# Output projection of the last chunk with the mixes as the stationary side

## The chip, the core and the metric

The kernel runs on one core of a Trainium2 chip. A core has a matrix engine (TensorE, PE in the profile; its loads of the stationary operand are shown as PEld), a vector engine (VectorE, DVE), a scalar engine (ScalarE, ACT), GpSimd (POOL) and SyncE (SP), which here only issues DMAs. Each of them works through its own queue in order; semaphores tie them together. The metric is the device time of one execution in microseconds (us); the profile comes from one execution of its own.

## The reference

One layer of a decoder with two groups of heads. For 1024 prompt tokens and 8 decode tokens (1032 rows in all, model width 2048) it computes an RMS norm, one wide input projection, sparse attention (1024 wide) and an mLSTM (1024 wide), gates both and sends them through one output projection:

```
mix = concatenate([attention * silu(z_att), mlstm_normed * sigmoid(o) * silu(z_ml)])   # (1032, 2048)
x   = x + mix @ w_out                                                                  # w_out (2048, 2048)
y   = x * rsqrt(mean(x * x, axis=-1) + 1e-6) * final_norm_w                            # final RMS norm
```

All of it is in float32. The caches, the attention and the mLSTM are not touched by the change and stay out here.

## The kernel before

Everything is kept transposed: features on the 128 partitions, tokens along the free dimension. `proj` (L1336) runs the input projection over 61 column tiles; lanes of jobs (L283 to L289) slip the attention and the mLSTM in between by weights and due times of their own. Both write to DRAM: the gates to `gateS`, attention to `attS`, the mLSTM to `hS`. After column tile 58 twelve of the sixteen mix row tiles (`PRE`) of the first token chunk are already made.

**float32 by halves.** A product of float32 operands is made from three matmuls: each operand is split into a high part H in the matrix format (a cast on ACT, L210) and a low part L (what the cast lost, a subtraction on DVE, L211); the products H·H, H·L and L·H are added in PSUM. `wload` and `wsplit` (L201, L215) load a weight tile of 128 x 512 numbers (256 KB) by one DMA on SP into a raw tile and make H and L of it. How far this runs ahead is set by the number of raw tiles and of pairs H, L in a pool: 2 and 3 in `wst`, 4 and 4 in `pb`.

**The output projection** (L1451 to L1483) walks through three token chunks `CB` = columns 0 to 387, 388 to 775, 776 to 1031. For each chunk `mixprep` makes the sixteen mix tiles (gate times branch output, split into mH and mL); those of `PRE` lie in pool `pb0`, used by chunks 0 and 2, the others in `pb`. Then for each of 16 tiles t of 128 output features, and four weight tiles of four row tiles each, 48 matmuls run with the **weights as the stationary side** (128 x 128) and the **mix as the moving side** (388 or 256 columns), L1470. The sum in one PSUM bank gets the residual added on DVE (L1475), is squared on ACT (L1478), and the squares are added up on GpSimd (L1480).

`finish` (L1430) ends a chunk. Because features lie on partitions, the sum of squares needs matmuls with a column of ones (`row_rstd`, L235), a power on GpSimd (L244), and transposes that spread the result over the partitions (L251, copied by L253). Then all 16 tiles y are scaled by norm weight and root (L1442; in the last chunk partly by ACT and GpSimd, L1444 and L1445) and stored to `yT` (L1446). `finish` is a generator: for chunks 0 and 1 it is advanced between the tiles t of the next chunk; for the last chunk it runs after everything else.

**What sets the order.** The code gives a program order; the framework then schedules each engine's queue against a simulated timeline, with everything under `tc.high_priority()` (weights) first. An instruction that is ready in that simulation may stand far ahead of its place in the code; the finished queues are then fixed and in order. Pools that are closed give their memory to later ones, and a tile on reused memory waits for the last reader of the old one.

Of the kernel before, what the change touches and what calls it, by code (L numbers as in the profile page):

```python
# [8 lines left out]
F32 = mybir.dt.float32  # L9
# [15 lines left out]
CB = ((0, 388), (388, 388), (776, 256))  # L25
CBN = 388
PRE = (8, 9, 10, 11, 12, 13, 14, 15, 0, 1, 2, 3)
# [110 lines left out]
def body(tc, A, stop=None):  # L138
# [62 lines left out]
    def wload(src, cols, pool, raws, bufs):  # L201
        raw = pool.tile([128, 4, 128], F32, name="wraw", bufs=raws)
        H = pool.tile([128, 4, 128], F32R, name="wH", bufs=bufs)
        L = pool.tile([128, 4, 128], F32R, name="wL", bufs=bufs)
# [10 lines left out]
    def wsplit(src, cols, pool, raws, bufs, tie=False):  # L215
        H, L, load, cast = wload(src, cols, pool, raws, bufs)
        dma = load(slice(0, 4))
        if tie:
            pin(dma)
        cast(slice(0, 4))  # L220
        return H, L

    evp = ctx.enter_context(tc.tile_pool(name="evp", bufs=6))
# [1072 lines left out]
    def mixload(ci, k, pool, tie=False):  # L1296
        c0, cn = CB[ci]
        nb = 2 if pool is not pb0 and k not in PRE else 1
# [124 lines left out]
    with tc.tile_pool(name="pb", bufs=2) as pb:  # L1423
        pre = PRE
        korder = pre + tuple(k for k in range(KT) if k not in pre)

        def ytile(ci, t):
            return pb.tile([128, CBN], F32, name=f"y{t}", bufs=2 if t < 3 else 1)[:, :CB[ci][1]]

        def finish(ci, ys, accs):  # L1430
            c0, cn = CB[ci]
            last = ci == len(CB) - 1
            rs = pb.tile([128, CBN], F32, name="rs", bufs=1)[:, :cn]
            rr = row_rstd(accs, rs, cn, pb)
            next(rr)
            yield
            for _ in rr:
                pass
            for t in range(KT):
                eng = G if last and t % 3 == 2 else V  # L1440
                if eng is V:
                    V.scalar_tensor_tensor(ys[t], ys[t], fnw[:, t:t + 1], rs, OP.mult, OP.mult)  # L1442
                else:
                    SC.activation(ys[t], ys[t], AF.Copy, scale=fnw[:, t:t + 1])  # L1444
                    G.tensor_tensor(ys[t], ys[t], rs, OP.mult)  # L1445
                (SC if last and t % 2 else SY).dma_start(A["yT"][t, :, c0:c0 + cn], ys[t])  # L1446
                if t % 4 == 3:
                    yield

        todo = None  # L1450
        for ci, (c0, cn) in enumerate(CB):  # L1451
            for k in korder:
                if mixb[ci][k] is None:
                    use0 = k in pre and ci % 2 == 0
                    mixprep(ci, k, pb0 if use0 else pb)
            ys = []
            acc = pb.tile([128, CBN], F32, name="acc", bufs=2)[:, :cn]
            for t in range(KT):
                p = bank()[:, :cn]
                n = 0  # L1460
                for q in range(4):
                    with tc.high_priority():
                        i = t * 4 + q
                        old = (ci == 0 and t == 0) or (i % 7) % 2 == 1
                        H, L = wsplit(A["wo"][t, q], 128, *((wst, 2, 3) if old else (pb, 4, 4)))
                    for k in range(4):
                        kk = korder[q * 4 + k]
                        mH, mL = mixb[ci][kk]
                        for w_, x_ in ((H, mH), (H, mL), (L, mH)):
                            PE.matmul(p, w_[:, k, :], x_, start=(n == 0), stop=(n == 47))  # L1470
                            n += 1
# [12 lines left out]
        for _ in todo:  # L1484
            pass
# [70 lines left out]
```

## Time and profile before

| What | Time |
|---|---|
| median of three runs | 2077.87 us (2075.32 to 2081.95) |
| the profiled execution | 2064.6 us |
| its span, first to last instruction | 2062.8 us |
| mean granted TensorE clock | 0.996 |
| TensorE matmuls busy | 2034.1 us (99%) |
| VectorE busy | 1215.2 us (59%) |
| ScalarE busy | 836.4 us (41%) |
| GpSimd busy | 331.5 us (16%) |
| DMA, mean over the span | 132 GB/s, 272.85 MB |

A row of a timeline gives start, duration, engine, line of the code, operation, output and inputs, shape, and in brackets the idle time before it and what ended it. Rows marked SPq are DMA issues, with the time the queue was occupied, not the time of the transfer. A matmul's duration includes its way through the array; consecutive ones overlap. A row of the groups gives count, busy time in us, mean of one in ns and, behind the second bar, the engine's idle time before them with its releasers.

### The profile page before, as it was taken

The numbers are of one execution on the slowest core, as the hardware profiler recorded it, in microseconds if no ns is written. First come the engines' busy times: TensorE is split into PE (matmuls) and PEld (weight loads), VectorE is DVE, ScalarE is ACT, GpSimd is POOL, SyncE is SP. The second block draws the span as 40 slices with busy tenths as digits, with TensorE's granted clock in tenths as the row PEclk, the third lists the DMA queues.
The fourth block names the chain that finished last, engine by engine and source line by source line (L and its number), as shares of the span: only waits on it lengthen the run. The fifth ranks groups of instructions, "written<-read, shape, count | busy, mean of one in ns | idle before, by whom it ended". The sixth has DMA issues, their size and how long they took to land.

```text
span 2062.8 us, 36440 instructions
## 1 busy us (share of the span) xinstructions
PE 2034.1 (99%) x13284; PEld 1999.7 (97%) x13284; DVE 1215.2 (59%) x3060; ACT 836.4 (41%) x1667; POOL 331.5 (16%) x405
## 2 busy tenths in 40 slices
PE   8999999999999999999999999989999999999997
PEld 8999999999999999999999999989999999999997
DVE  8332457556695876886455455356676467374464
ACT  8122244233531455312365555434454235343343
POOL 0002556600000000024011001012222111101011
PEclk9999999999999999999999999999999999999998
DMA  7444533322222212254322332256665758586584
GB/s 244 106 110 116 157 108 113 107 75 72 78 68 74 72 59 71 63 168 136 107 75 86 107 98 70 72 158 190 189 198 161 190 194 273 150 249 182 148 256 138
DMA packets 229777, 272.85 MB, mean 132 GB/s; under 512 B 36661, under 2 KB 162741, under 8 KB 229597
## 3 DMA queue, kind: packets, MB, share of 16 engines
q1 hardware_dynamic: 222381, 256.70, 42.0%
q0 software_dynamic: 5632, 12.59, 2.2%
q8 instruction: 104, 1.70, 0.4%
q10 hardware_dynamic: 1584, 1.23, 0.2%
q14 instruction: 76, 0.62, 0.1%
HBM read 210.54 MB, written 59.88 MB: 131 GB/s over the span
## 4 chain that ended last, share of the span: by engine, by line
PE 88%; DMA 4%; DVE 3%; ACT 1%; issue 1%; SPq 1%; POOL 0%; DVEq 0%; ACTq 0%; POOLq 0%
PE pj L1333 56%; PE bank L1470 17%; PE bank L441 3%; PE bank L636 2%; PE bank L585 2%; PE bank L627 2%; PE bank L935 1%; PE bank L1333 1%; DMA qk<-mlS 1%; DMA xr<-in_xT_dram 1%; DMA ev<-gateS 0%; DMA out_C_s_dram<-Cb 0%; PE bank L1053 0%; DVE wL L211 0%; DMA rb<-rowS 0%
## 5 line engine op out<-in xcount | busy, mean ns | idle before, releaser
L1333 PE MATMUL pj<-xH,wH 128*128 128x344 f32 (+2 forms) x2736 | 883.5, 324 | 6.3 <-ACT xH L261 3.2
L1333 PE MATMUL pj<-xL,wH 128*128 128x344 f32 (+2 forms) x2736 | 883.2, 323 | 0.2 <-DVE xL L262 0.2
L1333 PE MATMUL pj<-xH,wL 128*128 128x344 f32 (+2 forms) x2736 | 882.9, 323 | 0.0
L210 ACT CAST wH<-wraw 128x512 fp32r<-128x512 f32 (+2 forms) x439 | 267.6, 614 | 636.1 <-PE pj L1333 429.4
L1333 PEld LDWEIGHTS pj<-xH,wH 128*128 128x128 f32 (+1 forms) x2736 | 513.5, 188 | 10.6 <-ACT xH L261 4.8
L1333 PEld LDWEIGHTS pj<-xL,wH 128*128 128x128 f32 (+1 forms) x2736 | 513.4, 188 | 3.0 <-DVE xL L262 1.0
L1333 PEld LDWEIGHTS pj<-xH,wL 128*128 128x128 f32 (+1 forms) x2736 | 513.9, 188 | 2.0
L211 DVE TENSOR_TENSOR wL<-wraw,wH 128x512 fp32r<-128x512 f32 (+2 forms) x439 | 305.5, 700 | 350.6 <-ACT wH L210 338.3
L1470 PE MATMUL bank<-mH,wH 128*128 128x388 f32 (+1 forms) x768 | 245.0, 321 | 0.4 <-ACT wH L210 0.4
L1470 PE MATMUL bank<-mL,wH 128*128 128x388 f32 (+1 forms) x768 | 244.9, 319 | 0.0
L1470 PE MATMUL bank<-mH,wL 128*128 128x388 f32 (+1 forms) x768 | 244.4, 319 | 0.0
L922 POOL DMA_INDIRECT kp<-in_cik_dram,idx x128 | 128.6, 1005 | 105.6 <-PE bank L935 56.3
L1470 PEld LDWEIGHTS bank<-mH,wH 128*128 128x128 f32 x768 | 144.3, 188 | 0.7 <-ACT wH L210 0.6
L1470 PEld LDWEIGHTS bank<-mL,wH 128*128 128x128 f32 x768 | 144.5, 188 | 0.0
L1470 PEld LDWEIGHTS bank<-mH,wL 128*128 128x128 f32 x768 | 144.2, 188 | 0.0
L490 ACT ACTIVATE eq<-eq 128x512 bf16<-128x512 bf16 (+2 forms) x93 | 78.4, 843 | 113.7 <-DVE eq L489 113.4
L443 ACT ACTIVATE rl<-bank 128x512 f32<-128x512 f32 (+2 forms) x160 | 79.0, 522 | 79.5 <-PE bank L441 51.9
L446 DVE SCALAR_TENSOR_TENSOR s<-rl,wiN,s 128x512 f32<-128x512 f32 (+2 forms) x150 | 94.9, 654 | 21.5 <-ACT rl L443 18.4
L329 DVE TENSOR_TENSOR ev<-pj,rstd 128x344 f32<-128x344 f32 x144 | 73.6, 512 | 53.7 <-PE pj L1333 44.9
L632 DVE TENSOR_TENSOR ptL<-bank,ptH 128x512 fp32r<-128x512 f32 (+1 forms) x80 | 50.5, 635 | 64.3 <-ACT ptH L631 63.7
L1480 POOL TENSOR_TENSOR acc<-acc,sq 128x388 f32<-128x388 f32 (+1 forms) x42 | 43.1, 1025 | 280.3 <-ACT sq L1478 280.3
L332 POOL COPY dec<-ev 128x8 f32<-128x8 f32 x28 | 11.4, 406 | 475.9 <-DVE ev L329 198.9
(367 smaller groups left out, 2441.6 us busy)
## 6 DMA issues: line engine op xcount, KB each, us to landing
wraw<-in_wa_dram SPq DMA_DIRECT2D x238, 256.0 KB
wraw<-in_wo_dram SPq DMA_DIRECT2D x192, 256.0 KB
gateS<-ev SPq DMA_DIRECT2D x72, 172.0 KB
mlS<-ev SPq DMA_DIRECT2D x48, 172.0 KB
xr<-in_xT_dram SPq DMA_DIRECT2D x15, 516.0 KB
mL<-gateS SPq DMA_DIRECT2D x32, 194.0 KB
xr<-in_xT_dram SPq DMA_DIRECT2D x32, 194.0 KB
out_yT_dram<-y SPq DMA_DIRECT2D x32, 194.0 KB
```

The costliest lines, as they stand in the source:

```text
L210: a = SC.copy(H[:, s, :cols], raw[:, s, :cols])
L211: return a, V.tensor_tensor(L[:, s, :cols], raw[:, s, :cols], H[:, s, :cols].bitcast(F32), OP.subtract)
L329: V.tensor_tensor(e, ps[c][:cols, :cn], rstd[:cols, c0:c0 + cn], OP.mult)
L441: PE.matmul(p[:, :cn], qi[:, h % 4, :], ki[x][:, c0:c0 + cn], start=(x == 0), stop=(x == 1))
L443: SC.activation(r[:, :cn], p[:, :cn], AF.Relu)
L446: v = V.scalar_tensor_tensor(s[:, c0:c0 + cn], r[:, :cn], wv, s[:, c0:c0 + cn], OP.mult, OP.add)
L490: SC.activation(junk2[:, :W1], junk2[:, :W1], AF.Copy, accum_out=cnt[:, 1:2])
L632: V.tensor_tensor(pL[:, :kw], pt[:, :kw], pH[:, :kw].bitcast(F32), OP.subtract)
L922: g = G.indirect_dma_start(out=kp, out_offset=None, in_=A["cik"], in_offset=bass.IndirectOffsetOnAxis(ap=idx[:, m:m + 1], axis=0))
L1333: PE.matmul(ps[:cols, :cn], w_[:, k, :cols], x_[kk][:, c0:c0 + cn], start=(kk == 0 and z == 0), stop=(kk == 15 and z == 2))
L1470: PE.matmul(p, w_[:, k, :], x_, start=(n == 0), stop=(n == 47))
L1480: G.tensor_tensor(acc, acc, sq, OP.add)
```

## The change

The chunks are taken in another order, and the last one is computed in another orientation.

- `CB` becomes columns 256 to 643, 644 to 1031, 0 to 255. The first two chunks (the second with the decode tokens) run as before; the chunk taken last holds tokens 0 to 255.
- In that last chunk the **mixes are the stationary side** (128 features x 128 tokens) and the **weights the moving side** (128 features x 512 columns). The output lies with tokens on partitions. The loop runs over 4 column groups g of 512, in them over 16 row tiles n, and over 2 blocks b of 128 tokens: 6 matmuls of 512 columns per weight tile.
- The host adds a weight layout `wt` with one contiguous 128 x 512 tile per (g, n), the untransposed x of the 256 tokens (`x2`) and the final norm weights as a row (`fnr`, broadcast over partitions by one DMA). The output of these tokens is `yP`, untransposed.
- The sum of squares of a token is now a sum along the free dimension, taken by ACT with accum_out. Groups 0 to 2 are multiplied by the norm weights on GpSimd as they come; the root is made from the fourth group's sum, and then four tiles are scaled and stored per block, 256 KB each.
- In group 3 all sixteen weight pairs are kept (pool `pw`), so that block 0 runs first over all n and is closed while block 1 runs.
- Pools move: `evp` is closed before the output projection; the mixes of the first two chunks lie in `pm` (left side), those of the last in `pb0` and a new `pb1`; the tiles y and weight tiles of the first two chunks in `pb` on the right side. After chunk 1 `pm` is closed and `pt` (2 raw, 3 pairs, and the new chunk's tiles) takes its memory; after group 1 `pb` is closed and `pw` takes its.
- The remaining scalings of chunk 1 (`todo`) are advanced at every third n of groups 0 and 1, two tiles at a time. ACT and GpSimd no longer take part in `finish`.

```diff
-CB = ((0, 388), (388, 388), (776, 256))
+CB = ((256, 388), (644, 388), (0, 256))
+NT0 = 256
...
+    evctx.close()
+    pb1 = ctx.enter_context(tc.tile_pool(name="pb1", bufs=1, side="right"))
+    yctx, mctx = ExitStack(), ExitStack()
+    pb = yctx.enter_context(tc.tile_pool(name="pb", bufs=2, side="right"))
+    pm = mctx.enter_context(tc.tile_pool(name="pm", bufs=2))
...
+    def mixes(ci):
+        for k in korder:
+            if mixb[ci][k] is None:
+                mixprep(ci, k, (pm, pm, pb1)[ci] if ci == 1 or k not in PRE else pb0)
...
         for t in range(KT):
-                if t % 4 == 3:
+            if t % 2:
                 yield
...
+    mctx.close()
+    mixes(2)
+    pt = ctx.enter_context(tc.tile_pool(name="pt", bufs=1))
+    ss = pt.tile([128, 2, 8], F32, name="ss")
+    fnr = pt.tile([128, D], F32, name="fnr")
...
+    def block(p, b, n, H, L):
+        kk = korder[n]
+        mH, mL = mixb[2][kk]
+        bs = slice(b * 128, b * 128 + 128)
+        for x_, w_, z in ((mH, H, 0), (mL, H, 1), (mH, L, 2)):
+            PE.matmul(p, x_[:, bs], w_.rearrange("p a b -> p (a b)"), start=(n == 0 and z == 0), stop=(n == KT - 1 and z == 2))
+
+    def close(g, b, p):
+        y = res.pop(b)
+        V.tensor_tensor(y, p, y, OP.add)
+        jk = pt.tile([128, 512], F32, name="jk", bufs=2)
+        SC.activation(jk, y, AF.Square, accum_out=ss[:, b, g:g + 1])
+        yt[b][g] = y
+        if g < 3:
+            yt[b][g] = pt.tile([128, 512], F32, name=f"yt{b}{g}")
+            G.tensor_tensor(yt[b][g], y, fnr[:, g * 512:g * 512 + 512], OP.mult)
...
+        if g == 3:
+            V.tensor_scalar(ss[:, b, 5:6], ss[:, b, 3:4], 1.0 / D, ss[:, b, 4:5], OP.mult, OP.add)
+            G.tensor_tensor(ss[:, b, 6:7], ss[:, b, 5:6], mhalf, OP.pow)
+            rs = ss[:, b, 6:7]
+            SC.activation(yt[b][0], yt[b][0], AF.Copy, scale=rs)
+            SY.dma_start(A["yP"][b, :, 0:512], yt[b][0])
+            V.scalar_tensor_tensor(y, y, rs, fnr[:, 1536:2048], OP.mult, OP.mult)
+            SY.dma_start(A["yP"][b, :, 1536:2048], y)
+            SC.activation(yt[b][1], yt[b][1], AF.Copy, scale=rs)
+            SC.dma_start(A["yP"][b, :, 512:1024], yt[b][1])
+            V.tensor_scalar(yt[b][2], yt[b][2], rs, None, OP.mult)
+            SY.dma_start(A["yP"][b, :, 1024:1536], yt[b][2])
+
+    pw = None
+    for g in range(4):
+        ps = [bank() for b in range(2)]
+        ws = []
+        for n in range(KT):
+            with tc.high_priority():
+                if g < 3:
+                    H, L = wsplit(wslice(g, n), 128, *((wst, 2, 3) if n % 2 or not g and n < 6 else (pt, 2, 3)))
+                else:
+                    H, L = wsplit(wslice(g, n), 128, pw, 4, 1, tag=str(n))
+            if n == (2 if g == 3 else 10):
+                resid(g)
+            if n == 2 and not g:
+                SY.dma_start(fnr, A["fnr"].partition_broadcast(128))
+            block(ps[0], 0, n, H, L)
+            if g < 3:
+                block(ps[1], 1, n, H, L)
+            else:
+                ws.append((H, L))
+            if g < 2 and n % 3 == 1:
+                next(todo, None)
+        if g == 1:
+            for _ in todo:
                 pass
+            yctx.close()
+            pw = ctx.enter_context(tc.tile_pool(name="pw", bufs=1, side="right"))
+        with tc.high_priority():
+            close(g, 0, ps[0])
+        if g == 3:
+            for n, (H, L) in enumerate(ws):
+                block(ps[1], 1, n, H, L)
+        with tc.high_priority():
+            close(g, 1, ps[1])
...
+    a["x2"] = x[:NT0].reshape(2, 128, D)
+    a["fnr"] = npa(final_norm_w)
...
+    a["wt"] = wo.reshape(KT, 128, 4, 512).transpose(2, 0, 1, 3)
```

More of the change, by code (lines that the diff above doesn't have):

```diff
@@ L1297, in mixload @@
         c0, cn = CB[ci]
-        nb = 2 if pool is not pb0 and k not in PRE else 1
+        nb = 2 if ci < 2 and k not in PRE else 1
         h = pool.tile([128, CBN], F32R, name=f"mH{k}", bufs=nb)[:, :cn]
@@ L1421, in body @@
     xctx.close()
[L1423 to L1437, printed above, removed]
-                pass
[L1439 to L1446, printed above, removed]
-                if t % 4 == 3:
[L1448 to L1471, printed above, removed]
-                xr = pb.tile([128, CBN], F32, name="xr")[:, :cn]
-                SY.dma_start(xr, A["xT"][t, :, c0:c0 + cn])
-                y = ytile(ci, t)
-                V.tensor_tensor(y, p, xr, OP.add)
-                ys.append(y)
-                sq = pb.tile([128, CBN], F32, name="sq")[:, :cn]
-                SC.activation(sq if t else acc, y, AF.Square)
-                if 0 < t < KT - 1:
-                    G.tensor_tensor(acc, acc, sq, OP.add)
-                if todo and (t == 0 or t >= 2):
-                    next(todo, None)
-            todo = finish(ci, ys, (acc, sq))
-        for _ in todo:
-            pass
```

76 lines of the change are left out of this document (67 added, 9 removed).

## The prediction

> **What bounds the kernel now.** I read the page first, then the chain of waits over the last 380 us, then the timelines of the engines around the last chunk of the output projection and its end.
>
> ```profile
> PE 2034.1 (99%) x13284; PEld 1999.7 (97%) x13284; DVE 1215.2 (59%) x3060; ACT 836.4 (41%) x1667; POOL 331.5 (16%) x405
> PE 88%; DMA 4%; DVE 3%; ACT 1%; issue 1%; SPq 1%; POOL 0%; DVEq 0%; ACTq 0%; POOLq 0%
> PE pj L1333 56%; PE bank L1470 17%; PE bank L441 3%; PE bank L636 2%; PE bank L585 2%; PE bank L627 2%; PE bank L935 1%; PE bank L1333 1%; DMA qk<-mlS 1%; DMA xr<-in_xT_dram 1%; DMA ev<-gateS 0%; DMA out_C_s_dram<-Cb 0%; PE bank L1053 0%; DVE wL L211 0%; DMA rb<-rowS 0%
> ```
>
> TensorE is busy throughout, and the chain runs through its matmuls. So time leaves this kernel in three ways only: fewer or denser matmuls, a stall removed, a shorter end after the last matmul. The change touches the last chunk (256 tokens). Here are its first and last matmuls with a neighbour each, and its one stall, from TensorE's timeline:
>
> ```profile
> 1954.34 0.28 PE L1470 MATMUL bank<-mH,wH 128*128 128x256 f32 x1
> 2045.84 0.28 PE L1470 MATMUL bank<-mH,wH 128*128 128x256 f32 x1
> 2047.84 0.28 PE L1470 MATMUL bank<-mH,wL 128*128 128x256 f32 x1
> 1987.91 0.28 PE L1470 MATMUL bank<-mL,wH 128*128 128x256 f32 x1
> 1988.55 0.39 PE L1470 MATMUL bank<-mH,wH 128*128 128x256 f32 x1 [0.36 <-ACT wH L210]
> ```
>
> A row's duration includes pipeline time; what counts is the step from start to start. From 2045.84 to 2047.84 lie 17 steps (18 matmuls, of which the first and the last are shown): 0.1176 us each for 256 columns. The step at 1987.91 is 0.64 us, so about 0.5 us were lost there. The last matmul ends at 2048.12; the span ends at 2062.8. That end of 14.7 us is the second thing to see:
>
> ```profile
> 2048.16 0.42 DVE L1475 TENSOR_TENSOR y<-bank,xr 128x256 f32<-128x256 f32 x1 [5.24 <-PE bank L1470]
> 2048.68 0.42 ACT L1478 ACTIVATE sq<-y 128x256 f32<-128x256 f32 x1 [4.70 <-DVE y L1475]
> 2049.15 0.38 PE L235 MATMUL bank<-onesf,sq 128*128 128x1 f32 x2 [0.91 <-ACT sq L1478]
> 2050.25 0.71 POOL L244 TENSOR_TENSOR rr<-rr,mhalf 128x2 f32<-128x2 f32 x1 [5.93 <-DVE rr L240]
> 2051.49 0.42 DVE L253 COPY rs<-bank 128x256 f32<-128x256 f32 x1 [1.31 <-PE bank L251]
> 2051.95 6.87 DVE L1442 SCALAR_TENSOR_TENSOR y<-y,nw,rs 128x256 f32<-128x256 f32 x11
> 2053.02 6.00 SPq L1446 DMA_DIRECT2D out_yT_dram<-y  x8
> GB/s 0 0 0 0 0 0 0 0 0 22 0 0 0 0 0 98 265 309 333 44 238 208 350 254 46 295 306 344 344 336 347 372 344 342 336 85 0 0 0 0
> ```
>
> Sum over the partitions by matmul, root, transpose back, copy: the scale is ready 3.8 us after the last matmul. Then eleven scalings on VectorE (and some on GpSimd) feed 2.1 MB of output; the last row (40 slices of 2048 to 2063) has the stores running at about 344 GB/s until 2061.5, and 1.3 us more to the span's end.
>
> **The change, part by part.** *Matmuls.* 16 row tiles x 48 matmuls of 256 columns (768) become 4 column groups x 2 token blocks x 48 (384) of 512 columns. The same columns stream in all. L585 has single-core rows of 512 columns with a fresh stationary side each time, in this form:
>
> ```profile
> 1000.33 0.40 PE L585 MATMUL bank<-kH,qH 128*128 128x512 f32 x1
> 1001.71 0.84 PE L585 MATMUL bank<-kH,qL 128*128 128x512 f32 x3
> 1002.39 0.32 PE L1333 MATMUL pj<-xL,wH 128*128 128x344 f32 x1
> ```
>
> From the first row to the third lie nine matmuls (six single rows and the x3 one) in 2.06 us: 0.229 us each. 384 x 0.229 = 87.9 us against 768 x 0.1176 = 90.3 us: 2.4 us gained. The gain is half of the fixed part of each step. The Trainium skill ("TensorE: Matmul & The Clock Gate", back-to-back issue gap) states a step of columns/2.4 GHz plus 2.5 ns; by it the gain would be 768 x 109.2 - 384 x 215.8 ns, an estimate of 1.0 us. The rows show 117.6 and 229 ns, so I keep 2.4. With the stall of 0.5 us gone the matmul part gives 2.9 us.
>
> *The end.* The sum of squares now comes per token from accum_out, tokens lie on partitions, and so neither sums nor transposes on TensorE remain. Three of four column groups are already weighted by GpSimd beforehand, and the first token block is closed while 48 matmuls (11 us) of the second run. Prices:
>
> ```profile
> L601 ACT ACTIVATE pP<-pP,st 128x512 f32<-128x512 f32 x40 | 28.6, 717 | 6.0 <-DVE st L598 6.0
> L598 DVE TENSOR_SCALAR st<-st 128x1 f32<-128x1 f32 x64 | 9.0, 148 | 0.1
> L446 DVE SCALAR_TENSOR_TENSOR s<-rl,wiN,s 128x512 f32<-128x512 f32 x75 | 55.6, 748 | 14.2 <-ACT rl L443 12.5
> L454 DVE TENSOR_SCALAR s<-rl,wiN 128x512 f32<-128x512 f32 x3 | 1.5, 484 | 1.0 <-ACT rl L443 1.0
> L210 ACT CAST wH<-wraw 128x512 fp32r<-128x512 f32 x430 | 264.1, 618 | 635.8 <-PE pj L1333 429.4 <-PE bank L1470 142.5 <-DMA wraw<-in_wa_dram 25.2
> L211 DVE TENSOR_TENSOR wL<-wraw,wH 128x512 fp32r<-128x512 f32 x430 | 301.8, 705 | 348.3 <-ACT wH L210 336.1 <-DMA bd<-iqD 5.0 <-PE bank L1470 3.3
> ```
>
> After the last matmul: add 0.70 (as L211), square with accumulation 0.72 (L601), scalar step 0.15 (L598), root 0.71 (L244), with some 0.3 us of handovers: 2.6 us. Then ACT scales two tiles (0.62 each, L210), DVE one weighted (0.75, L446) and one plain (0.48, L454). The first is ready at 3.2, the last at 3.9 us. Four stores of 256 KB make 1.05 MB: at 344 GB/s 3.05 us. The first old store was issued at 2053.02 and bytes flow from about 2053.7; so flow starts about 0.7 us after 3.3, ends at 7.1, and with the 1.3 us seen at the close the end is 8.4 us. 14.7 - 8.4 = **6.3 us** gained. Bounds: 7.3 us if stores overlap the scalings perfectly, 4 us if the four stores run at the 200 to 250 GB/s of some slices.
>
> *The weights.* 64 tiles of 256 KB stay, with one SP load, one ACT and one DVE cast each; in both host layouts a partition's row of a tile is 2 KB in one piece. A tile now lasts 6 x 0.229 = 1.37 us on TensorE (before 12 x 0.1176 = 1.41). What shrinks is the buffering: 6 raw tiles and 7 split pairs before, 4 and 6 now, and in the first six tiles of group 0 only 2 and 3, since the new buffers overlay the mixes that the previous chunk reads to its end. With four raw tiles a load may take 4 x 1.37 - 0.62 - 0.71 = 4.1 us from issue to landing. The only landing on the chain:
>
> ```profile
> 1983.88 0.56 DVE wL L211
> 1984.45 3.41 DMA wraw<-in_wo_dram
> 1987.88 0.63 ACT wH L210
> ```
>
> 3.4 us, below 4.1, while stores ran beside it. So the steady state holds with 0.7 us spare.
>
> *Group 0.* Here the leftover of the previous chunk meets the thin buffers. In the old kernel it looked so, on DVE and SP:
>
> ```profile
> 1974.12 0.67 DVE L211 TENSOR_TENSOR wL<-wraw,wH 128x512 fp32r<-128x512 f32 x1
> 1974.71 8.04 DVE L1442 SCALAR_TENSOR_TENSOR y<-y,nw,rs 128x388 f32<-128x388 f32 x14
> 1982.68 0.67 DVE L211 TENSOR_TENSOR wL<-wraw,wH 128x512 fp32r<-128x512 f32 x1
> 1974.82 0.33 SPq L207 DMA_DIRECT2D wraw<-in_wo_dram  x1
> 1975.84 8.51 SPq L1446 DMA_DIRECT2D out_yT_dram<-y  x14
> 1984.45 0.45 SPq L207 DMA_DIRECT2D wraw<-in_wo_dram  x1
> 1980.00:1985.00 5.00, 5.00 (x45) 5.00 (x44) 1.00 1.03 369
> ```
>
> Fourteen scalings and stores in one run, no weight load for 9.6 us, at 369 GB/s on the DMA engines (last column of the last row). The cover was twelve tiles deep and only 0.5 us was lost. The scheduler, not the place of the yields, made that run, so I expect one again. Traffic of group 0, if all stores fall there: 16 weight tiles (4.2 MB), 16 stores of 198 KB (3.2), the broadcast norm weights (128 x 8 KB, 1.05), residuals (0.5): 8.9 MB, which at 369 GB/s take 24.2 us against 22.0 us of matmuls. I charge the difference, **2.2 us**. Bounds: 0 if the tiles loaded ahead hide it, 6 us below.
>
> *Group 3.* Its first block needs 16 tiles in 48 x 0.229 = 11 us, 381 GB/s, above 369. But it has 16 pairs of its own, and in group 2 DMA has 369 - 191 (256 KB per 1.37 us) = 178 GB/s to spare over 22 us: 3.9 of the 4.2 MB. DVE's 16 casts (11.3 us) likewise fit into the spare half of group 2. I charge 0.3 us, bounds 0 and 4 (all 16 loaded late, at DMA rate behind SP's earlier loads).
>
> *The rest.* GpSimd loses fourteen sums and gets six products; at 16% of the span busy it keeps nobody waiting. The chunks before now start at column 256, with the same matmuls. Their pools move: the mixes of rows 4 to 7 overlay the evacuation buffers of the input projection, so SP may hold at its head for the last gate stores. Cover: in the old run these rows' products are first made 10 us into the chunk, with TensorE not waiting. I charge 0; bounds -0.3 (as much gained, if the new order happens to suit) and 3 (one store's landing, as above).
>
> ```profile
> 1680.50 0.34 PE L1470 MATMUL bank<-mH,wH 128*128 128x388 f32 x1
> 1690.90 0.56 DVE L1313 TENSOR_TENSOR mx<-mL,mH 128x388 f32<-128x388 f32 x1
> ```
>
> **Sum.** -2.9 - 6.3 + 2.2 + 0.3 = -6.7 us. On the profiled execution (span 2062.8, its own time 2064.6) that is 2056.1 and 2057.9. That execution lies 13.3 us under the median of the runs, 2077.9; taking the difference over gives **2071.2 us**.
>
> **Rivals.** (1) *Group 0 starves.* The run of scalings (8 us without a low-part cast) starts with about four split tiles ahead instead of six: 5.5 us of matmuls against 8.0 + 1.3. TensorE stalls 3.9 us more than charged: 2075.1. For it: in-order DVE and SP, the thin first six tiles. Against: the casts have priority, and the stores are now yielded in twos. The Trainium skill ("TensorE: Matmul & The Clock Gate", the HAM clock gate) says that an idle window of some 3.4 us halves the TensorE clock for as long again; by it such a stall would cost an estimated 1.7 us more. Here the granted clock was below 1.00 only in the idle end (0.65, the third number from the right), which agrees but shows no stall of that length.
>
> ```profile
> 2048.00:2063.00 15.00, 1.50 (x12) 1.09 (x10) 7.88 (x14) 0.42 (x1) 4.88 (x6) 0.65 0.42 140
> ```
>
> (2) *Slower: four raw tiles don't carry the weights.* If landing rises to 5.5 us under the stores, broadcast and early loads of group 3, a tile takes (5.5 + 1.33)/4 = 1.71 us instead of 1.37; over 48 tiles 16 us, 2084.9. It decides against the change from a mean landing of 4.9 us, where 48 x 0.19 us eats the 9.2 us gained. For it: 369 GB/s is the most these rows show, and the landing of 3.4 us was measured with one queue. Against: old casts wait mostly for TensorE, not for DMA:
>
> ```profile
> L210 ACT CAST wH<-wraw 128x512 fp32r<-128x512 f32 x177 | 108.5, 619 | 157.0 <-PE bank L1470 139.4 <-DMA wraw<-in_wo_dram 14.7 <-issue 1.1
> ```
>
> By the Trainium skill ("DMA: Bandwidth & Descriptors", anatomy) a DMA takes 2.0 us plus bytes/436 GB/s, an estimate of 2.6 us for a tile, and this rival falls; the measured 3.4 us says less room. (3) *It doesn't do what it says:* 512-column steps cost twice the 256-column ones, 0.235 us: 2.4 us less, 2073.6. Against: the L585 rows.
>
> **How the numbers follow.** Forecast 0.48; rival 1 0.25; rival 2 0.16; rival 3 0.08; 0.03 for an end much shorter than worked out (2067). A measurement of this kernel tells about 0.3% (6.2 us) from no change. The forecast and the short end count as faster, with a little of the forecast's own spread at the edge taken off: 0.49. Rivals 1 and 3 and that edge: 0.34 same. Rival 2, and a group 0 that stalls and throttles: 0.17 slower. The range 2064 to 2084 takes in the short end and the bounds of the charged costs (-9.2 us: 2068.7; the runs before spread +-3 us), and rival 2 nearly to its price.
>
> **What would show it.** Right: 384 matmuls of 128x512 stepping 0.229 us; end 8 to 9 us; idle of TensorE in the last 95 us of 2 to 3 us, at group 0. Wrong: idle above 5 us released by the weight casts, landing above 4.1 us, or casts in groups 1 and 2 waiting for DMA rather than for TensorE; an end above 10 us; idle at the start of the first chunk.

## The result and the profile after

The changed kernel takes **2087.41 us** (median of 17 runs, 2082.84 to 2092.86) where the kernel before takes 2079.4 us (17 runs beside them): a ratio of **1.0039, 95% interval 1.0029 to 1.005**. It is slower by about 8 us, 0.4%. The forecast was 2071.2 us.

The two profiled executions, 2064.6 us before and 2087.62 us after, differ by 23 us, and most of that is not the change. The first matmul of the output projection starts at 1680.5 us in the one and at 1696.4 us in the other, though everything up to there is the same work. The stage from that matmul to the span's end is what the change touches, and it repeats well, so it is the measure from here on:

| Kernel | projection starts | chunks 1 and 2 of it | last chunk | after the last matmul | projection to end |
|---|---|---|---|---|---|
| before | 1680.50 | 273.84 | 93.78 | 14.68 | 382.30 |
| after | 1696.39 | 274.52 | 105.96 | 8.93 | 389.41 |

The stage is 7.1 us longer, which is the measured 8 us within its interval (6.0 to 10.4 us). The end got 5.75 us shorter; the last chunk got 12.2 us longer.

First the page of after: TensorE's busy line, and the chain of waits by engine.

```profile
PE 2040.7 (98%) x12890; PEld 1983.2 (95%) x12890; DVE 1213.3 (58%) x3050; ACT 836.2 (40%) x1666; POOL 323.9 (16%) x393
...
PE 84%; DMA 4%; DVE 4%; issue 3%; ACT 2%; another core or an unknown queue 1%; SPq 1%; POOL 0%; POOLq 0%; ACTq 0%; DVEq 0%
```

The busy share barely moves (98% for 99%), since 12 us are lost in 2086. But TensorE's share of the chain fell from 88 to 84%, and VectorE and ScalarE, which hand the weights over, and issue gained. The waits of TensorE within the last chunk (total us, times, longest) name the same two:

```profile
PE bank L1506 <- ACT wH L211: 6.9, 6, 4.0
PE bank L1506 <- DVE wL L212: 3.6, 2, 2.3
```

Where in the chunk? TensorE's timeline gives the first matmul of each group of 96 by count, then the one before group 3's second block, and the last matmul of all:

```profile
1970.91 0.40 PE L1506 MATMUL bank<-wH,mH 128*128 128x512 f32 x1
...
2004.71 0.40 PE L1506 MATMUL bank<-wL,mH 128*128 128x512 f32 x1
...
2032.21 0.40 PE L1506 MATMUL bank<-wL,mH 128*128 128x512 f32 x1
...
2054.49 0.39 PE L1506 MATMUL bank<-wL,mH 128*128 128x512 f32 x1
...
2065.37 0.40 PE L1506 MATMUL bank<-wL,mH 128*128 128x512 f32 x1
...
2076.47 0.40 PE L1506 MATMUL bank<-wL,mH 128*128 128x512 f32 x1
```

From 2065.37 to 2076.47 lie 48 steps: 0.231 us each, 22.2 us for a group of 96. So group 0 lasts 33.8 us (11.5 too many), group 1 27.5 us (5.3 too many), and groups 2 and 3 lose nothing. The biggest loss of group 0 is seen in TensorE's timeline, and the granted clock (third number from the right) in two windows of 5 us around it; the last two numbers are the busy share of the DMA engines and GB/s:

```profile
1984.11 0.59 PE L1506 MATMUL bank<-wH,mH 128*128 128x512 f32 x1 [3.98 <-ACT wH L211]
1984.50 0.63 PE L1506 MATMUL bank<-wH,mL 128*128 128x512 f32 x1
...
1987.49 0.53 PE L1506 MATMUL bank<-wL,mH 128*128 128x512 f32 x1
1987.86 0.39 PE L1506 MATMUL bank<-wH,mH 128*128 128x512 f32 x1
```

```profile
1980.00:1985.00 5.00, 1.02 (x4) 0.73 (x5) 3.70 (x7) 1.17 (x2) 0.00 (x0) 0.94 1.00 366
1985.00:1990.00 5.00, 4.63 (x15) 3.38 (x13) 5.00 (x10) 1.76 (x3) 0.00 (x0) 0.72 0.98 328
```

TensorE waits 4.0 us, and the nine matmuls behind the wait take 3.75 us instead of 2.1, in a window whose mean granted clock is 0.72. The Trainium skill ("TensorE: Matmul & The Clock Gate", the HAM clock gate) says that an idle window of about 3.4 us halves TensorE's clock until a busy one of that length has passed; the row agrees. So the idle stretch costs more than its own length, here 1.7 us more. What was it waiting for? The issues of SP from the turn of the chunks on:

```profile
1959.63 12.28 SPq L208 DMA_DIRECT2D wraw<-in_wt_dram  x5
1971.95 0.43 SPq L1547 DMA_DIRECT2D fnr<-in_fnr_dram  x1
1972.43 1.38 SPq L1499 DMA_DIRECT2D xr<-in_x_dram  x3
1973.91 2.23 SPq L208 DMA_DIRECT2D wraw<-in_wt_dram  x2
1976.19 0.50 SPq L1499 DMA_DIRECT2D xr<-in_x_dram  x1
1976.78 3.31 SPq L208 DMA_DIRECT2D wraw<-in_wt_dram  x2
1981.41 2.32 SPq L1448 DMA_DIRECT2D out_yT_dram<-y  x4
1984.81 0.34 SPq L208 DMA_DIRECT2D wraw<-in_wt_dram  x1
1985.34 5.14 SPq L1448 DMA_DIRECT2D out_yT_dram<-y  x9
...
1993.34 19.43 SPq L208 DMA_DIRECT2D wraw<-in_wt_dram  x22
```

The broadcast norm weights (1 MB) and three residual tiles (0.8 MB), neither wanted before group 0 ends, stand in SP's queue ahead of the weight tile of 1973.91. During the wait the DMA engines are full (1.00 of the time at 366 GB/s in the window shown); at that rate 1.8 MB take an estimated 4.9 us. The chain of waits says what that does to it, and shows the run of scalings on VectorE as the next link:

```profile
1973.91 9.43 DMA wraw<-in_wt_dram
...
1983.44 0.63 ACT wH L211
...
1986.91 2.29 DVE y L1447 x5
```

9.4 us from issue to landing, against 3.4 us for the one landing on the chain of the kernel before. The Trainium skill ("DMA: Bandwidth & Descriptors", queues, rings and completion order) says that each DMA engine takes the descriptors of a queue in the order of its ring; the row agrees. The 22 loads from 1993.34 on hold tiles of group 3 between those of group 1: the finished queue has them there, far ahead of their place in the code.

### The profile page after: what moved, and what is told of

It reads as the page before. It is cut to its first block, busy times and chain, and to the rows that moved or that the text cites. A ratio compares the mean times of both kernels' runs of the same rounds, so it can differ in the third digit from the quotient of the medians.

```text
span 2085.8 us, 35541 instructions
## 1 busy us (share of the span) xinstructions
PE 2040.7 (98%) x12890; PEld 1983.2 (95%) x12890; DVE 1213.3 (58%) x3050; ACT 836.2 (40%) x1666; POOL 323.9 (16%) x393
## 4 chain that ended last, share of the span: by engine, by line
PE 84%; DMA 4%; DVE 4%; issue 3%; ACT 2%; another core or an unknown queue 1%; SPq 1%; POOL 0%; POOLq 0%; ACTq 0%; DVEq 0%
PE pj L1335 54%; PE bank L1470 13%; PE bank L443 3%; PE bank L638 2%; PE bank L587 2%; PE bank L1506 2%; PE bank L629 2%; DMA wraw<-in_wt_dram 1%; PE bank L1335 1%; DVE wL L212 1%; PE bank L937 1%; DMA xr<-in_xT_dram 1%; DMA qk<-mlS 1%; PE bank L828 1%
## 5 line engine op out<-in xcount | busy, mean ns | idle before, releaser
L1470 PE MATMUL bank<-mH,wL 128*128 128x388 f32 x512 | 173.6, 339 | 0.1
L1470 PE MATMUL bank<-mL,wH 128*128 128x388 f32 x512 | 173.5, 339 | 0.0
L1470 PE MATMUL bank<-mH,wH 128*128 128x388 f32 x512 | 172.7, 339 | 0.0
L1470 PEld LDWEIGHTS bank<-mH,wL 128*128 128x128 f32 x512 | 96.1, 188 | 0.4 <-DVE wL L212 0.4
L1470 PEld LDWEIGHTS bank<-mH,wH 128*128 128x128 f32 x512 | 96.2, 188 | 0.3 <-ACT wH L211 0.2
L1470 PEld LDWEIGHTS bank<-mL,wH 128*128 128x128 f32 x512 | 96.2, 188 | 0.0
L443 PE MATMUL bank<-ki,qi 128*128 128x512 f32 (+2 forms) x320 | 76.0, 358 | 2.5 <-ACT rl L445 2.5
```

The costliest lines, as they stand in the source:

```text
L443: PE.matmul(p[:, :cn], qi[:, h % 4, :], ki[x][:, c0:c0 + cn], start=(x == 0), stop=(x == 1))
```

## The experiments

My theory after this: no buffer or bandwidth is short on the average; transfers and instructions that could wait stand in bursts ahead of the weights in in-order queues. The rival is the prediction's own second one: four raw tiles don't carry the weights. All numbers below are of the same stages; a table at the end has them together.

**The kernel before once more**, to see what the input stage does by itself.

> The kernel before, once more, for a second profile of it. In the changed kernel's profile the output projection began at 1696.6 us, in the one of before at 1680.5 us, although the queues of all engines are the same up to there. Theory: the input stage simply varies from execution to execution; then this profile begins the output projection between 1688 and 1698 us with a span of 2072 to 2082 us, and first matmul of the projection to the end of the span is 382 us again (within 2 us). Rival: the change slows the input stage (other addresses in DRAM); then this profile gives 1680 to 1683 us again.

The projection started at 1701.2 us, 20.7 us later than in the first execution of the same kernel and later than even the range expected (1688 to 1698); the stage took 382.34 us (382.30 before). So a difference of two spans says little here, and for this kernel the stage repeats to 0.1 us. The later profiles show that the start goes with the chip they ran on: on each of five chips the kernels of this document start the projection within 4 us of each other, at 1681 to 1683 us on two of them and at 1693, 1695 to 1698 and 1701 to 1704 us on the others.

**One cause at a time.** Norm weights and residuals later (`pin` holds an instruction at its place in the program's order):

```diff
-            SY.dma_start(res[b], ...)
+            pin(SY.dma_start(res[b], ...))
-            if n == 2 and not g:
-                SY.dma_start(fnr, ...)
+            if n == 14 and not g:
+                pin(SY.dma_start(fnr, ...))
```

> The broadcast norm weights and the residual loads (1.8 MB) keep their place in program order behind the weight tiles of group 0 instead of being issued ahead of them. The last chunk (first 512-column matmul to the end of the last matmul) took 105.9 us in the changed kernel. Queue theory (these loads stand in front of the weight tiles in SP's in-order queue and in the DMA rings): the stall of 4.0 us at 1984 and the slow clock behind it go, last chunk 99 to 101 us. Rival (four raw tiles are too few whatever the order): the stall moves, last chunk 104 to 107 us.

Last chunk 102.10 us, 3.9 less: between the two expectations. The wait of 4 us is gone, but others took part of its place; what TensorE waits for in this kernel:

```profile
PE bank L1506 <- DVE wL L212: 3.6, 3, 2.7
PE bank L1506 <- ACT wH L211: 3.3, 3, 1.6
```

Group 3's weight loads held behind group 2's:

```diff
-                    H, L = wsplit(wslice(g, n), 128, pw, 4, 1, tag=str(n))
+                    H, L = wsplit(wslice(g, n), 128, pw, 4, 1, True, tag=str(n))
```

> Only the sixteen loads of group 3 are held to program order, so that they are issued behind those of group 2 and not among those of group 1. Queue theory: the stalls of group 1 (1.4 us at 2012 and about 1.5 us at 2021, and 0.8 us before) go, last chunk 101 to 103 us instead of 105.9; the first block of group 3 may then wait up to 2 us. Rival (few raw tiles): casts of group 1 wait for DMA as before and the last chunk stays at 105 to 107 us.

Last chunk 104.39 us, 1.6 less, short of the expectation. Group 1 falls from 27.5 to 22.2 us, so the early loads were all of its loss; but group 3's first block grows from 11.1 to 15.0 us. The loss of 5.3 us was exchanged for one of 3.9.

Chunk 1's stores issued by GpSimd instead of SP:

```diff
-            SY.dma_start(A["yT"][...], ys[t])
+            (G if ci else SY).dma_start(A["yT"][...], ys[t])
```

> Only the sixteen stores of the second chunk go to GpSimd's DMA queue instead of SP's, so no weight load waits behind a store whose scaling is still to come. Same bytes. If it is the order in SP's queue: the stall around 1991 to 1997 (2.3 and 0.4 us, and the casts' wait of 6.9 us for DMA) goes, last chunk 101 to 104 us. If it is the bytes (stores and loads share the same DMA engines): 105 to 107 us, the stall only moves. If it is VectorE's run of scalings: TensorE still waits some 2 us for a low-part cast there.

Last chunk 103.35 us, 2.6 less, as expected for the order in SP's queue. The wait behind the run of scalings stayed (2.3 us), as expected too.

**More buffers** for the even weight tiles: `(pt, 2, 3)` becomes `(pt, 4, 4)`.

> Only the buffers of the weights in the last chunk grow: the even tiles' pool from two raw tiles and three pairs to four and four; orders of the other transfers as the compiler then makes them. Theory of the queue (norm weights, residuals, stores and early loads of group 3 stand ahead of weight loads in SP's in-order queue): the last chunk falls from 106.0 only to 101 to 105 us, and TensorE still waits over 2 us at its start. Rival 2 of the prediction (too few raw tiles, whatever the order): it falls to 93 us or less, with no gap above 1 us.

Last chunk 109.65 us, 3.7 *more*: both expectations missed. Buffers alone don't help; but with the larger pool the compiler also chose other orders, so this run does not isolate them.

**The three edits together.**

> The three edits of the earlier runs together: norm weights loaded at the fifteenth tile of group 0, group 3's weight loads held in program order, chunk 1's stores issued on GpSimd's queue. If the three causes are separate, their gains add (4.3 + 2.1 + 2.5 us): projection to end 380 to 381 us, last chunk 96 to 98 us. If they only pass the same wait on to each other: no better than the norm weights alone, 385 us, and the wait for VectorE's low parts (2.3 us and more) remains, since its run of scalings is left as it is.

Last chunk 102.73 us, no better than the first edit alone: the additive theory fell here. What is removed in one place returns in another; the longest wait is now 3.4 us for a low part, behind VectorE's run of scalings.

**The scalings to GpSimd.** ScalarE weights y in chunk 1, GpSimd multiplies by the root and stores; the late loads as before. Then three variants: the first with more buffers; the first with GpSimd's stores right behind each product; and this last one with eight of group 3's tiles loaded during group 2 as well:

```diff
-            V.scalar_tensor_tensor(ys[t], ys[t], fnw[:, t:t + 1], rs, OP.mult, OP.mult)
+            if ci:
+                G.tensor_tensor(ys[t], ys[t], rs, OP.mult)
...
+                if g == 2 and n % 2:
+                    ahead[n // 2] = wsplit(wslice(3, n // 2), 128, pw, 4, 1, True, tag=str(n // 2))
```

> As the run before, and the sixteen scalings of chunk 1 leave VectorE: ScalarE weights y behind its square during the chunk, GpSimd multiplies by the root and issues the store. Theory (queue order and the run of scalings, not the number of buffers): no wait of TensorE for low parts above 0.5 us, last chunk 91 to 94 us, projection to end 374 to 378 us, and the time 5 to 8 us (0.2% to 0.4%) under the kernel before. Rival (four raw tiles don't carry the weights at all): last chunk stays above 98 us, no gain over the kernel before.

> As the run before, and four raw tiles and four pairs instead of two and three for the even tiles. Theory: with the orders mended the buffers matter little, within 1 us of the run before (last chunk 90 to 93 us). Rival 2: 3 us or more better than the run before.

> As the run with GpSimd scaling and late loads, but GpSimd's instructions are held in program order, so that each store of chunk 1 follows its own scaling instead of seven and three in a burst. Theory (bursts in front of the weights): the wait of 2.8 + 1.1 us in group 1 and the half-rate matmuls behind it go, the last chunk falls from 100.4 to 94 to 96 us; the 2 to 3 us at the start of group 3 stay. Rival (the DMA engines cannot carry stores and weights of groups 0 and 1 together, whatever the order): no better than 99 us, the wait moves.

> As the run before, and eight of group 3's sixteen weight tiles are loaded during group 2, one behind every second tile. Theory: the 2 to 3 us at the start of group 3 go too, last chunk 91 to 94 us, projection to end 374 to 377 us, 5 to 8 us below the kernel before in the stage; the time 0.1% to 0.4% below it. Rival (four raw tiles of the pool do not carry a tile every 0.7 us): the wait in group 3 stays, or moves into group 2.

Last chunk 100.44, 102.72, 103.14 and 102.24 us: the theory's expectation missed in all four; what came was the rival's in the first (above 98 us), the third (99 us or more) and the last (a wait that stays in group 3). Against the kernel before they measured 1.0026 (1.0013 to 1.0039), 1.003 (1.0017 to 1.0044), and the last 1.0019 (1.001 to 1.0028); the third has a single run. One reason stands in the timelines of the third of them, where GpSimd multiplies (1.04 us, last row) and issues a store every 1.9 us:

```profile
1971.10 14.68 DVE L212 TENSOR_TENSOR wL<-wraw,wH 128x512 fp32r<-128x512 f32 x9 [1.62 <-ACT wH L211]
...
1984.50 0.68 DVE L212 TENSOR_TENSOR wL<-wraw,wH 128x512 fp32r<-128x512 f32 x1
...
1986.33 0.69 DVE L212 TENSOR_TENSOR wL<-wraw,wH 128x512 fp32r<-128x512 f32 x1 [0.55 <-ACT wH L211]
...
1975.26 1.04 POOL L1448 TENSOR_TENSOR y<-y,rs 128x388 f32<-128x388 f32 x1
```

Nine low-part casts take 14.7 us. The first seven each overlap a product on GpSimd and take 1.9 to 2.0 us; the eighth (second row) and the ninth don't and take 0.68 us, like the next one alone. The work taken off VectorE came back: in the last of the four its casts take 58.9 us in all, against 47.5 us in the version below that keeps the scalings on VectorE, where these take 9.9 us. The Trainium skill ("GPSIMD Engine Reference", specifications) says that the two engines share their way to SBUF and get in conflict where VectorE reads two SBUF inputs, as this subtraction does; the trace agrees. This can be the reason for groups 0 and 1 alone, where GpSimd multiplies. In the last of the four, 6.6 of the 13.1 us above the later floor of 89.2 us lie in groups 2 and 3, where the casts wait for weight loads that come late; why they come late was not tried.

**No stores of chunk 1**, in the changed kernel otherwise untouched.

> The changed kernel without the sixteen stores of chunk 1's y (the output of 388 tokens is left unwritten; the scalings stay). If the order in SP's queue and the wait of the late pool for the stores' completion are the main part, the last chunk falls from 106.0 to 98 to 101 us: the first stall of 4 us behind the norm weights stays, the one behind the run of scalings (2.3 us) stays, everything behind the stores goes. If DMA bandwidth in sum is the cause: below 96 us, since 3.2 of group 0's 8.9 MB are gone.

Last chunk 104.28 us, a miss for both: group 0 keeps its 33.9 us (33.8 with the stores), though 3.2 of its 8.9 MB are gone; group 1 gains 1.7 us. So neither traffic in sum nor the stores made group 0 slow.

**The floor.** Nothing but weights in the last chunk: the kernel leaves out the residuals, the norm weights and the finish of chunk 1 with its output. The second run loads eight tiles of group 3 during group 2.

```diff
-            SY.dma_start(res[b], ...)
-        V.tensor_tensor(y, p, y, OP.add)
+        V.tensor_copy(y, p)
-                SY.dma_start(fnr, ...)
+                G.memset(fnr, 1.0)
-                next(todo, None)
+                pass
```

> The changed kernel with nothing in the last chunk but its weights: no residuals (not added), norm weights set to one by GpSimd, chunk 1's sum, scalings and stores left out (its output unwritten), group 3's loads in program order. Rival 2 (four raw tiles don't carry the weights): stalls all along, last chunk 97 us or more. Theory: groups 0 to 2 run without a stall at 0.231 us a step, only group 3's first block waits, 2 to 4 us; last chunk 91 to 93 us.

> As the run before, with eight of group 3's weight tiles loaded during group 2. Theory: the wait in group 3 goes, last chunk 89 to 90.5 us, the floor of 384 steps of 0.231 us plus at most 1.5 us. If four raw tiles in that pool are too few, it stays within 1 us of the run before.

Both: **89.16 us**, and TensorE has no wait at all in the chunk. That is better than both expectations of the first run (91 to 93 us by the theory, since group 3 was to wait; 97 us or more by the rival). Its first and last matmul in the former, and two windows (the last number is GB/s):

```profile
1956.74 0.40 PE L1505 MATMUL bank<-wH,mH 128*128 128x512 f32 x1
...
2045.50 0.40 PE L1505 MATMUL bank<-wL,mH 128*128 128x512 f32 x1
```

```profile
1957.00:1977.00 20.00, 20.00 (x88) 16.14 (x87) 11.13 (x17) 9.97 (x17) 1.78 (x1) 1.00 0.62 199
1977.00:1997.00 20.00, 20.00 (x88) 16.23 (x87) 12.97 (x17) 10.35 (x19) 3.01 (x2) 1.00 0.67 211
```

383 steps in 88.76 us: 0.2318 us each. Two raw tiles and three pairs in each of the two pools carry the weights, from the first tile of group 0 to group 3's first block. That settles the rival as far as the weights alone go: the buffers are enough until something gets between. Now one thing at a time is put back: the loads of norm weights and residuals, where the changed kernel has them; and the finish of chunk 1 without its stores.

> The last chunk with its weights and, beside them, only the loads of norm weights and residuals at the places in SP's queue that the changed kernel gives them (chunk 1's sum, scalings and stores left out, its output unwritten; group 3's loads in program order). Theory: 1.8 MB ahead of the weights cost the first stall and the half-rate matmuls behind it, last chunk 89.2 + 4 to 7 us = 93 to 96 us. If only the sum of all traffic does harm: under 91 us.

> The last chunk with its weights and, beside them, only chunk 1's sum and its scalings on VectorE (no stores: chunk 1's output unwritten; no residuals, norm weights set to one; group 3's loads in program order). Fourteen scalings stand in one run in VectorE's queue, 8 us. Theory: one stall of 2 to 4 us, last chunk 91.5 to 94 us, and no later one. If the tiles loaded ahead ride it out: under 90.5 us.

The loads alone cost **8.7 us** (97.86). SP's issues and TensorE's wait in that kernel:

```profile
1967.94 0.43 SPq L1547 DMA_DIRECT2D fnr<-in_fnr_dram  x1
1968.42 1.38 SPq L1499 DMA_DIRECT2D xr<-in_x_dram  x3
1969.90 2.25 SPq L208 DMA_DIRECT2D wraw<-in_wt_dram  x2
```

```profile
1979.21 0.79 PE L1506 MATMUL bank<-wH,mH 128*128 128x512 f32 x1 [5.14 <-ACT wH L211]
1979.80 0.63 PE L1506 MATMUL bank<-wH,mL 128*128 128x512 f32 x1
1980.23 0.63 PE L1506 MATMUL bank<-wH,mH 128*128 128x512 f32 x1
```

Four transfers ahead of two weight tiles: 5.1 us of waiting, then thirteen steps in 5.6 us instead of 3.0. That makes 7.9 us in group 0; 0.8 us more are lost in group 3. The finish without stores costs **6.8 us** (95.96). VectorE's run in that kernel:

```profile
1983.37 0.68 DVE L212 TENSOR_TENSOR wL<-wraw,wH 128x512 fp32r<-128x512 f32 x1
1983.96 7.55 DVE L1447 SCALAR_TENSOR_TENSOR y<-y,nw,rs 128x388 f32<-128x388 f32 x14
1991.44 0.68 DVE L212 TENSOR_TENSOR wL<-wraw,wH 128x512 fp32r<-128x512 f32 x1
```

Fourteen in one run, 8.1 us between two casts; TensorE loses 2.1 us there. Another 2.3 us are the matmuls of chunk 1's sum and transposes (which the kernel before has in its last chunk too), and 2.4 us are lost later, mostly in group 3's first block. My expectations for the two (93 to 96 and 91.5 to 94) were short by 2 us each: in the first the stall with the slow steps behind it was taken too short, in the second the sum's matmuls and the later losses were left out. 89.16 + 8.70 + 6.80 = 104.7 us, and the kernel without stores measured 104.28. The totals agree to 0.4 us, but not group by group: the sum puts 34.7 us into group 0 (33.9 without stores), 23.1 into group 1 (25.8) and 24.5 into group 3 (22.2). In these runs group 3's loads keep the program's order, in the kernel without stores they come early among those of group 1. So the two causes account for group 0, and the agreement of the totals is in part luck.

**Spread instead of moved.** The scalings stay on VectorE but in program order; stores on GpSimd's queue, loads late, eight tiles of group 3 ahead, as above. Then the same with more buffers, and with loads and scalings later still:

```diff
-            V.scalar_tensor_tensor(ys[t], ys[t], fnw[:, t:t + 1], rs, OP.mult, OP.mult)
+            v = V.scalar_tensor_tensor(ys[t], ys[t], fnw[:, t:t + 1], rs, OP.mult, OP.mult)
+            if ci:
+                pin(v)
```

> Norm weights late, stores on GpSimd's queue, eight of group 3's weight tiles loaded during group 2, and the sixteen scalings stay on VectorE but in program order: runs of six and then two instead of one run of thirteen or more. Theory (every stall is a burst in front of the weights' way, on SP, on VectorE or on the port that GpSimd shares with it): no wait for low parts above 1.5 us, last chunk 93 to 97 us, projection to end 377 to 380 us. Rival (too few buffers for the sum of what runs in groups 0 and 1): 99 us or more, as in the runs before.

> As the run before, with four raw tiles and four pairs instead of two and three for the even tiles. If both causes act together, bursts and too few tiles to ride them out: 3 us or more below the run before, last chunk 90 to 93 us, and the time 0.2% to 0.4% below the kernel before. If buffers do not matter: within 1 us of the run before.

> As the run with spread scalings on VectorE (last chunk 94.7 us), with residuals and norm weights of group 0 three and one tiles later and one turn of scalings later. Theory: the 1.6 and 1.6 us lost in the first 16 us halve, last chunk 92 to 94 us, projection to end 375 to 377 us, time 0.2% to 0.4% below the kernel before. Rival (later traffic only meets group 1 and the late pool's wait for the stores): 95 us or more.

The first gives a last chunk of 94.73 us and a stage of 377.65 us, as the theory expected, and in time 2061.19 us against 2064.02: **0.9987 (0.9978 to 0.9996), faster than the kernel before**, by 0.13%. Against the three edits together (102.73 us), 3.7 of the 8.0 us gained lie in group 0, where the scalings are spread, and 4.8 in group 3, whose tiles come ahead; group 2, which loads them, loses 1.0. All that TensorE still waits for in its last chunk:

```profile
PE bank L1508 <- ACT wH L211: 1.5, 2, 0.8
PE bank L1508 <- DVE wL L212: 0.7, 1, 0.7
```

With more buffers it is 99.27 us and 1.0009 (1.0 to 1.0018), with everything later 96.77 us and 1.0002 (0.9991 to 1.0012). The former missed both of its expectations: one wait of 3.6 us came with the other order. The latter went the rival's way.

| Kernel | last chunk | projection to end | time against before |
|---|---|---|---|
| before | 93.8 | 382.3 | 1 |
| after | 106.0 | 389.4 | 1.0039 |
| loads late / group 3 late / stores on GpSimd | 102.1 / 104.4 / 103.4 | 385.1 / 387.3 / 386.9 | |
| the three together | 102.7 | 386.1 | |
| more buffers | 109.7 | 393.1 | |
| scalings on GpSimd; + buffers; + stores in turn; + group 3 ahead | 100.4; 102.7; 103.1; 102.2 | 383.8; 385.6; 386.4; 385.3 | 1.0026; 1.003; -; 1.0019 |
| no stores | 104.3 | 386.8 | |
| weights alone; group 3 ahead | 89.2; 89.2 | 371.3; 371.3 | |
| weights and loads; weights and finish | 97.9; 96.0 | 380.5; 378.2 | |
| scalings spread; + buffers; later | 94.7; 99.3; 96.8 | 377.7; 382.3; 380.0 | 0.9987; 1.0009; 1.0002 |

## Why the prediction was wrong

- **The failed step is group 0**: "8.9 MB, which at 369 GB/s take 24.2 us against 22.0 us of matmuls. I charge the difference, 2.2 us", bounds 0 and 6. Group 0 lost 11.5 us, 9.2 without the sum's matmuls. It was no question of bytes in sum. The DMA engines were busy 92% of group 0 at 305 GB/s, but with 3.2 MB fewer it lost the same, and in the spread version, where these bytes come in another order, it took 25.5 us instead of 33.8. It was the order: 1.8 MB that nobody needed yet went ahead of weight tiles when only two raw tiles were open, and cost 7.9 us of group 0 by themselves. The working counted these bytes but not whom they stand in front of, though the diff shows the norm weights at n = 2; the residuals stand at n = 10 there, and the finished queue had them beside the norm weights.
- *Rival 1* (the run of scalings) did occur, with a loss of 2.1 us when alone instead of 3.9; the halved clock it warned of came behind the other stall: nine steps in 3.75 us instead of 2.1, 1.7 us lost, which is the estimate.
- *Group 3* was charged 0.3 us, bounds 0 and 4. It cost 5.3 us, but in group 1: the loads ran too early, not too late. Held back they cost 3.9 us, the bound. With the weights alone they cost nothing. The prediction had used spare bandwidth of group 2 and had not asked when the scheduler would place these loads.
- *The end:* 8.4 us forecast, 8.93 measured, gain 5.75 for 6.3. The rows of after follow the working step by step:

```profile
2076.90 0.69 DVE L1510 TENSOR_TENSOR xr<-bank,xr 128x512 f32<-128x512 f32 x1 [7.47 <-PE bank L1506]
2077.62 0.63 ACT L1512 ACTIVATE jk<-xr 128x512 f32<-128x512 f32 x1 [8.01 <-DVE xr L1510]
...
2078.67 0.55 POOL L1523 TENSOR_TENSOR ss<-ss,mhalf 128x1 f32<-128x1 f32 x1 [10.43 <-DVE ss L1522]
2079.26 0.72 ACT L1525 ACTIVATE yt<-yt,ss 128x512 f32<-128x512 f32 x1 [0.91 <-POOL ss L1523]
...
2080.91 0.41 SPq L1532 DMA_DIRECT2D out_yP_dram<-yt  x1
```

- *Matmuls:* forecast 0.229 us a step and 2.4 us gained; at the floor 0.2318 us, 89.2 us for all, 1.2 us gained. Nine steps of another stage were too few for a difference of 1%. The two steps, 0.1176 us for 256 columns and 0.2318 for 512, leave a fixed part of 3.4 ns, and 384 of these are the 1.3 us at stake. The estimate of 1.0 us by the Trainium skill ("TensorE: Matmul & The Clock Gate", back-to-back issue gap) was nearer than the forecast, though its step of 215.8 ns is not seen here.
- *The rest*, charged 0: chunks 1 and 2 took 0.7 us longer.
- *Rival 2* named 2084.9 us and the result was 2087.4, and its signs appeared: of the five landings on the chain of after in groups 0 and 1 four took 4.3 to 9.4 us, over the 4.1 us that the working allowed, and ScalarE's casts in the last chunk waited mostly for DMA (first row, after) and no longer for TensorE (second row, before; total us, times, longest):

```profile
ACT wH L211 <- DMA wraw<-in_wt_dram: 31.8, 21, 8.0
ACT wH L210 <- PE bank L1470: 31.8, 40, 2.2
```

  But as many raw tiles were enough elsewhere: they ran 384 matmuls without a wait when only weights moved, and with all loads and stores spread they lost 3.3 us (94.73 less 89.16 and less 2.3 of sums). The casts' wait for DMA is no sign by itself either: in the spread version it is 35.6 us. A near time proves no cause.
- *Two small readings:* 369 GB/s is not quite the most that the prediction's rows show (a slice at the end has 372), and the landing that it set as the bound for chunks 1 and 2 is a load's, not a store's. Neither moves a term.
- *The balance:* matmuls -1.2, old stalls -1.2 (93.8 less 90.3 of matmuls and 2.3 of sums), end -5.75, group 0 +9.2, group 1 +5.3, chunks 1 and 2 +0.7: +7.1 us, the whole. Between the forecast (-6.7) and this lie 13.8 us: 7.0 from group 0, 5.0 from group 3's loads, 0.7 from chunks 1 and 2, and about 0.5 each from the end and from the matmuls with the old stalls.

Two things stay open. How much the number of buffers matters *beside* other traffic was not isolated, since each larger pool also changed the compiler's orders. And the timed ratios of the new versions lie 1 to 3.5 us above what their stage alone gives (the first GpSimd version: stage +1.5 us, time +5 us, 2.7 to 8.1); by subtraction the input stage added it. On the chip of the second profile of before, three changed kernels began the projection 1.6 to 2.6 us later than before did, one execution each; why was not tried.

## What to carry to other kernels

Sum of traffic against time says whether a stage can be fed; it does not say that it will be. Where few buffers are open, list for each in-order queue (the DMA issuer's, and each engine's that prepares operands) what stands ahead of the next critical item, when it is really needed, and how long it takes in one run; a load that is needed late belongs late in the queue. An idle stretch of 4.0 us on TensorE cost 5.7 us here, and a bulk elementwise task moved to GpSimd can slow VectorE by more than it relieves it (here by 11.4 us of longer casts for 9.9 us of scalings).

## What the runs showed of the hardware

- The same kernel before had medians of 2079.4, 2064.35, 2064.02 and 2076.66 us on four chips, and its two profiled executions began the projection at 1680.5 and 1701.2 us. In these two the difference lies in the input stage; from the projection on they agree to 0.04 us.
- VectorE's 128x512 subtraction from SBUF takes 0.69 us alone, and 1.9 to 2.0 us in the seven cases shown where GpSimd multiplies a 128x388 tile meanwhile.
- After waits of 4.0 and 5.1 us, steps of 512 columns took 0.43 us instead of 0.23, for 3.8 and 5.6 us. The length of the wait alone does not decide it in these traces: after 2.7 us with only the loads late eight steps were slow, after 3.4 us in the three edits together none was.
